# FFN middle of a two-layer decoder trunk: four parts in program order against five parts laid out by the kernel's own planner

## The chip, the cores and the metric

The kernel runs on one core of one Trainium2 chip. The metric is the device time of one execution in microseconds (us). Beside it stands one profiled execution, whose trace shows every instruction of the engines: TensorE (PE, with its weight loads as PEld), VectorE (DVE), ScalarE (ACT), GpSimd (POOL), and the DMA queues that SyncE (SP) and POOL issue.

## What is computed

Two layers of a decoder trunk, each a mixer (attention, two convolution groups, an output projection) followed by a feed-forward network (FFN). Only the FFN is touched:

```python
def ffn_sublayer(h, pre_g, post_g, w_up, conv_w, w_down):
    u = rms_norm(h, pre_g)
    z = jnp.einsum("bld,df->blf", u, w_up)
    z = causal_depthwise_conv(z, conv_w)
    g, up = jnp.split(z, 2, axis=-1)
    y = jnp.einsum("blf,fd->bld", jax.nn.silu(g) * up, w_down)
    return h + rms_norm(y, post_g)
```

The length is 528 (512 and 16 meta tokens), the model width 1024 (8 blocks of 128), the FFN width 2816, which is 22 blocks f of 128. For each f there is a gate half and an up half. All of it is float32, done as three matmuls on a high and a low part (hi times hi, hi times lo, lo times hi).

## The kernel before, in words

**Layout.** Channels lie on partitions, positions on the free axis. A weight block is loaded from DRAM into a raw tile (`raw` or `u`), ScalarE casts it to its high part (`whi`, `shi`, `ahi`), and VectorE subtracts to get the low part (`wlo`, `slo`, `alo`). A matmul takes 128x128 of such a weight and 264 columns of the right side (258 in the last layer, where some positions fall away). One product of 128 x 512 by 264 columns is 4 x 3 = 12 matmuls.

**Parts.** The 22 blocks are worked in parts (`PARTS`): 6, 6, 5, 5. In each part the up projections come first, then the gate (convolution taps, SiLU, product, split into `yhi` and `ylo`), and then the down projection: 8 output tiles m, each summing over the f of the part and added to `yp`. A down tile of a part of n blocks is 6n matmuls of 264 columns in layer 0 and 3n of 512 columns in layer 1.

**Seven products for eight.** The first part and the last block (f = 21) use plain up products. The 15 blocks f = 6 to 20 (`sevens`) cut the gate weight and the up weight into halves of 512 rows, and positions into two halves, so that eight block products become seven. The seven products of a block are a11, a12, s4, s2, a22, s3, s1 (`product`, `seven`, `p3`, `p4`), 84 matmuls in all. Their weights are sums of the loaded halves. The four sums are made by DMAs with an adding write, which POOL issues (`add1`, `add2`, `add3`): on the gate tile `raw` from DRAM, on the up tile `u` from DRAM, on `u` from `raw`, and on `raw` from `u`. The third needs the first, the fourth needs the third, and the gate tile must have been split before its first sum is added. After the sums, ScalarE and VectorE split the four results. There are two `u` tiles, and three `raw` tiles, which the down weights and the plain up weights use too. A `u` tile may be loaded again when its block's last sum has been added and its splits are done.

**The right sides.** t1, t2 and t4 are combinations of the pieces of the normed input, built during part 0 (`build_terms`). After the `yield "last"` t3 is built and the input itself, now scaled, is split again into `uhi` and `ulo`.

**What sets the order.** In this stretch the code is written in program order, with small pieces set ahead by hand (`ahead`, `AHEAD_STEPS`: load, split and add for the next block at named places), and a scheduler with a timeline then orders each engine's instructions at build time. Elsewhere (the mixer, and `finish`, which does the last part's down projection, the norm and the first products of what follows) the kernel uses its own planner, `Flow`: operations are given with an engine, a cost, what they wait for and a priority, matmul work is given as threads, and the planner simulates and so fixes the order (`manual_schedule`). Each engine, and each DMA queue, then works strictly in that order.

Lines of the profile: L648 are all matmuls of `mm3` (plain up and down products), L1978 those of the seven products. L1941/L1942 split the weights of the seven, L488/L489 other weights, L1915/L1916 split the input, L1998 to L2033 take the products out of PSUM into the z tiles, L1809 to L1836 are the convolution and gate, L2079/L2081 take the down tiles out, L1957/L1958/L1961/L1964 are the four adding DMAs.

## Time and profile before

| what | us |
|---|---|
| median of 3 runs | 1430.88 (1430.63 to 1435.54) |
| the profiled execution: its own time, its span | 1430.35, 1428.6 |
| PE busy, share of the span | 1289.2, 90% |
| layer 0, first down matmul of part 0 to last plain up product | 345.9 to 667.2 (321.3 long) |
| layer 1, the same | 1050.9 to 1372.4 (321.5 long) |
| DVE busy in the two stretches | 183.24 and 180.65 |
| ACT busy in the two stretches | 141.03 and 137.71 |

A row of the waits view gives engine, tile and line, what released it, and then the total, the number and the longest of the waits. A row of the timeline gives start, length, engine, line, operation, out<-in, shapes, and in brackets the idle time before it with what ended that. A row of the windows view gives the busy time of each engine with the number of instructions, then the granted TensorE clock as a share of full speed, the DMA share and GB/s. Matmuls overlap in the pipe, so one matmul's length in a row is longer than the distance between two.

### The profile page before, as it was taken

The page shows a single profiled execution, that of the slowest core. Times are in us where ns is not written, and L with a number is a line of the kernel's source. Part 1 is how long each engine was busy: PE and PEld are TensorE (multiplying, and loading weights), DVE is VectorE, ACT ScalarE, POOL GpSimd, SP SyncE. Part 2 cuts the span into 40 slices and gives each one's busy share as a digit, 9 for nine tenths or more (in the row PEclk, how much of TensorE's full clock was granted, in tenths as well). Part 3 has the DMA queues.
Part 4 walks back from the last instruction along what each step waited for, and adds up shares of the span by engine and source line. Part 5 has one row for each costly group of instructions (what it writes and reads, how often), then busy time and mean ns, then how long its engine had stood idle before and what let it go on. Part 6 is the DMA issues. An engine that isn't in the chain of part 4 may idle for free.

```text
span 1428.6 us, 24192 instructions
## 1 busy us (share of the span) xinstructions
PE 1289.2 (90%) x9390; PEld 1216.5 (85%) x9390; DVE 965.3 (68%) x1722; ACT 751.9 (53%) x1507; POOL 209.3 (15%) x387
## 2 busy tenths in 40 slices
PE   6999999999988889888989999999999788888886
PEld 6988989998988889888879898899978777777885
DVE  5688885799356546656666888668983555565565
ACT  7256677655344335345652566866553443443443
POOL 1312320000121021020003233100002110210200
PEclk9999999999999999999989999999999999999998
DMA  5133213432456366365240322153326653664641
GB/s 201 46 93 81 76 45 126 143 121 70 122 126 154 89 149 142 95 157 155 90 136 19 110 61 90 45 168 133 95 70 131 128 148 84 144 158 102 148 124 60
DMA packets 67219, 158.41 MB, mean 111 GB/s; under 512 B 7344, under 2 KB 21680, under 8 KB 66592
## 3 DMA queue, kind: packets, MB, share of 16 engines
q1 hardware_dynamic: 49184, 124.59, 27.1%
q0 software_dynamic: 17376, 31.73, 13.7%
q8 instruction: 74, 1.21, 0.4%
q10 hardware_dynamic: 544, 0.54, 0.1%
q14 instruction: 41, 0.34, 0.1%
HBM read 128.09 MB, written 8.65 MB: 96 GB/s over the span
## 4 chain that ended last, share of the span: by engine, by line
PE 47%; DMA 19%; DVE 14%; issue 8%; ACT 7%; POOL 4%; POOLq 0%; DVEq 0%; SPq 0%; ACTq 0%
PE psum L648 34%; DMA raw<-u 6%; DMA raw<-in_w_dram 6%; DMA u<-raw 4%; DMA u<-in_w_dram 3%; PE psum L1978 3%; PE psum L1397 2%; DVE c L1811 2%; PE psum L1146 2%; PE psum L1340 1%; PE psum L762 1%; DVE cacc L895 1%; DVE wlo L617 1%; ACT shi L1941 1%; POOL u L1961 1%
## 5 line engine op out<-in xcount | busy, mean ns | idle before, releaser
L648 PE MATMUL psum<-uhi,whi 128*128 128x264 f32 (+1 forms) x1024 | 276.1, 293 | 12.2 <-ACT uhi L805 10.1
L648 PE MATMUL psum<-ulo,whi 128*128 128x264 f32 (+1 forms) x1024 | 269.6, 287 | 1.9 <-DVE ulo L806 1.9
L648 PE MATMUL psum<-uhi,wlo 128*128 128x264 f32 (+1 forms) x1024 | 268.8, 286 | 0.0
L648 PE MATMUL psum<-yhi,whi 128*128 128x264 f32 (+3 forms) x824 | 237.5, 317 | 30.5 <-ACT yhi L1835 29.4
L648 PE MATMUL psum<-ylo,whi 128*128 128x264 f32 (+3 forms) x824 | 235.0, 311 | 2.3 <-DVE ylo L1836 1.8
L648 PE MATMUL psum<-yhi,wlo 128*128 128x264 f32 (+3 forms) x824 | 233.5, 309 | 0.7 <-DVE wlo L489 0.5
L648 PEld LDWEIGHTS psum<-uhi,whi 128*128 128x128 f32 x1024 | 185.6, 191 | 17.6 <-ACT uhi L805 10.9
L648 PEld LDWEIGHTS psum<-ulo,whi 128*128 128x128 f32 x1024 | 185.8, 191 | 2.9 <-DVE ulo L806 2.4
L648 PEld LDWEIGHTS psum<-yhi,whi 128*128 128x128 f32 x824 | 150.6, 195 | 44.1 <-ACT yhi L1835 31.9
L648 PEld LDWEIGHTS psum<-uhi,wlo 128*128 128x128 f32 x1024 | 185.7, 191 | 0.0
L648 PEld LDWEIGHTS psum<-ylo,whi 128*128 128x128 f32 x824 | 151.6, 195 | 11.1 <-DVE ylo L1836 4.3
L648 PEld LDWEIGHTS psum<-yhi,wlo 128*128 128x128 f32 x824 | 151.5, 194 | 7.4 <-DVE wlo L489 1.0
L1811 DVE SCALAR_TENSOR_TENSOR c<-z,pv,c 128x528 f32<-128x528 f32 (+1 forms) x176 | 130.5, 754 | 18.0 <-ACT c L1809 16.7
L617 DVE TENSOR_TENSOR wlo<-raw,whi 128x1024 fp32r<-128x1024 f32 (+2 forms) x86 | 99.2, 1168 | 34.9 <-ACT whi L613 34.7
L613 ACT CAST whi<-raw 128x1024 fp32r<-128x1024 f32 (+2 forms) x86 | 85.4, 1004 | 37.8 <-PE psum L648 21.9
L1942 DVE TENSOR_TENSOR slo<-raw,shi 128x512 fp32r<-128x512 f32 x60 | 40.8, 690 | 92.8 <-ACT shi L1941 88.2
L488 ACT CAST whi<-raw 128x768 fp32r<-128x768 f32 (+2 forms) x66 | 55.9, 846 | 87.1 <-PE psum L648 63.4
L1941 ACT CAST shi<-raw 128x512 fp32r<-128x512 f32 x60 | 35.6, 619 | 105.1 <-DMA raw<-u 70.5
L489 DVE TENSOR_TENSOR wlo<-raw,whi 128x768 fp32r<-128x768 f32 (+2 forms) x66 | 63.9, 969 | 36.8 <-ACT whi L488 34.7
L895 DVE SCALAR_TENSOR_TENSOR cacc<-apad,pv,cacc 128x528 f32<-128x528 f32 x120 | 87.6, 768 | 0.4
L1978 PE MATMUL psum<-h,shi 128*128 128x264 f32 (+1 forms) x240 | 53.5, 316 | 29.4 <-ACT shi L1941 21.3
L1941 ACT CAST shi<-u 128x512 fp32r<-128x512 f32 x60 | 37.0, 617 | 76.4 <-DMA u<-raw 76.0
(281 smaller groups left out, 3133.4 us busy)
## 6 DMA issues: line engine op xcount, KB each, us to landing
raw<-in_w_dram SPq DMA_DIRECT2D x114, 512.0 KB
u<-in_w_dram SPq DMA_DIRECT2D x30, 512.0 KB
raw<-in_w_dram SPq DMA_DIRECT2D x32, 384.0 KB
raw<-in_w_dram SPq DMA_DIRECT2D x32, 320.0 KB
u<-in_w_dram POOLq DMA_DIRECT2D x30, 256.0 KB, 4.0
raw<-in_w_dram POOLq DMA_DIRECT2D x30, 256.0 KB, 4.8
u<-raw POOLq DMA_DIRECT2D x30, 256.0 KB, 4.1
raw<-u POOLq DMA_DIRECT2D x30, 256.0 KB, 3.3
```

Of the source, the lines that this page charges most:

```text
L488: nc.scalar.copy(hi[:, :sz], raw[:, :sz])
L489: nc.vector.tensor_sub(lo[:, :sz], raw[:, :sz], hi[:, :sz].bitcast(F32))
L613: nc.scalar.copy(box["hi"][:, :sz], box["raw"][:, :sz])
L617: nc.vector.tensor_sub(lo[:, :sz], box["raw"][:, :sz], box["hi"][:, :sz].bitcast(F32))
L648: nc.tensor.matmul(d, lhsT=w[a][:, k, cols], rhs=rhs(b, k, hf), start=start and i == 0 and p == 0, stop=stop and i == n - 1 and p == 2)
L895: nc.vector.scalar_tensor_tensor(conv[j], in0=src, in1=conv[j], scalar=col("a_dw_w", CK * j + i), op0=ALU.mult, op1=ALU.add)
L1146: nc.tensor.matmul(ps[:n, :nw], lhsT=(uhi, ulo)[ui][:, k, P * b:P * b + n], rhs=w[wi][:, k % 4, :], start=k == 0 and p == 0, stop=k == KD ...
L1397: nc.tensor.matmul(acc[:, s0 - qa:qz - qa], lhsT=vt[:, b].rearrange("p h d -> p (h d)")[:, o:o + P], rhs=pt, start=b == 0 and i == 0, stop ...
L1811: nc.vector.scalar_tensor_tensor(dst, in0=src[:, i:i + 2 * fw], scalar=wtap(i, t), in1=dst, op0=ALU.mult, op1=ALU.add)
L1941: nc.scalar.copy(hi, raw)
L1942: nc.vector.tensor_sub(lo, raw, hi.bitcast(F32))
L1978: nc.tensor.matmul(d, lhsT=unit(f).a[a][i][:, P * k:P * (k + 1)], rhs=terms[b][j][k], start=start and k + p == 0, stop=k == KH - 1 and p = ...
```

## The change

The parts become 6, 3, 3, 3, 7. Everything from the end of part 0's plain products to `finish` is now laid out by the planner, in one plan with `finish`. Two threads feed PE: `ups`, the seven products of blocks 6 to 20 in the same order as before, and `downs`, the 8 down tiles of each of the first four parts, so one tile at a time. A list `goals` says after how many block products each down tile falls due: those of part 0 at 0, 0, 0, 0, 2, 5, 8, 11, and those of a later part spread evenly over the block products that follow its last block, the first 10 products later. A product waits while a due down tile can go. The weights, sums and splits of all 15 blocks are given to the planner at once, with priority by block. The tiles of the sums are kept and written again, instead of being allocated per block: each of s1 to s4 has one pair, a22 two, the gate split two, `u` two, gate raw three (one of them lent to part 0's down weights first), and down weights of the middle parts get one raw tile of their own (`draw`). t3 and the second split of the input, `late_terms`, are planned operations now. The last plain block and its gate run inside the same plan as `finish` (`last_up`). `finish` sums over 7 blocks instead of 5. The gate of block 5 is still scheduled by the build-time scheduler; the planner assumes it ready 7.5 us after its start. In the last layer 48 matmuls more are issued, since `finish` takes 2 x 256 columns where the middle takes 512.

```diff
-PARTS = (6, 6, 5, 5)
+PARTS = (6, 3, 3, 3, 7)
...
-                yield "last"
...
+            def late_terms():
...
+                terms["t3"] = [[t[k // 2][:, k % 2] for k in range(KH)] for t in t3]
+                plain_terms()
+                start, us = Tok(flow.now), 2 * sw
+
+                def unit_u(k):
+                    hi, lo, y = (t[:, k:k + 2, i0:] for t in (uhi, ulo, yp))
+                    n = 2 * (L - i0)
+                    a = act(act_us(n), lambda: nc.scalar.copy(hi, y), start, prio=0.1)
+                    return [a, dve(dve_us(n), lambda: nc.vector.tensor_sub(lo, y, hi.bitcast(F32)), a, prio=0.1)]
+
+                u_at = [unit_u(k) for k in range(0, KD, 2)]
+                ready_at["b11"], ready_at["b21"] = u_at[0] + u_at[1], u_at[2] + u_at[3]
...
+            sevens = list(range(PARTS[0], NF - 1))
+            ends = [sum(PARTS[:p + 1]) for p in range(len(PARTS))]
...
+                def __init__(self, f, bufs):
+                    self.a, self.box, self.at, self.slot = {}, {}, {}, {}
+                    box, src = self.box, [up_chunk(f, e) for e in range(2)]
+                    gs, us = Slot(), Slot()
+                    w = 1 + 0.001 * f
+                    lg = load_op(bufs["g"], gs, box, "g", src[0], 2 * HALF, w)
+                    lu = load_op(bufs["u"], us, box, "u", src[1], 2 * HALF, w)
+
...
+                    self.at["a11"] = self.at["a12"] = g2[1]
+
+                    def add(out, in_, *after):
+                        return gp(ADD_US, lambda: nc.gpsimd.dma_start(out(), in_(), accum_op=ALU.add), *after, prio=w, lat=ADD_LAT)
+
+                    def split(name, raw, *after):
+                        self.slot[name] = Slot()
+                        t = split_op(box, name, raw, after, bufs[name], self.slot[name], HALF, w)
+                        self.at[name] = t[1]
+                        return t
+
+                    a2 = split("a22", ub, lu)
+                    c1 = add(ua, lambda: src[1][:, HALF:], lu)
+                    c3 = add(ga, lambda: src[1][:, :HALF], *g2)
+                    c2 = add(ub, ga, c3, *a2)
+                    c4 = add(gb, ub, c2, *g2)
+                    s = {n: split(n, raw, c) for n, raw, c in (("s3", ga, c3), ("s1", ua, c1), ("s2", ub, c2), ("s4", gb, c4))}
+                    gs.close(s["s3"][1], s["s4"][1], c2)
+                    us.close(s["s1"][1], s["s2"][1], c4)
...
+            def ups(units, bufs):
+
+
+                def product(bank, f, a, b, *waits, start=False):
+                    u = units[f]
+                    yield [When(lambda: None if len(down_at) < due(counted[0]) and down_can() else [Tok(0.0)])]
+                    counted[0] += 1
+                    yield [u.at[a], *ready_at.get(b, []), *waits]
+                    d = psum[:, bank, :sw]
+                    w = u.weight(a)
+                    for k in range(KH):
...
+                def p3(f):
+                    d, tok = yield from product(banks_of(f)[0], f, "s4", "b22", done[f, "u4"])
+                    copied(f, "c12", 0, 1, d, tok)
+                    conv_flow(f, 0, [done[f, "c11"], done[f, "c12"]])
...
+                    zg, zu = (z_free.get((f - 2, e), []) for e in range(2))
+                    d, tok = yield from product(ba, f, "a11", "b11", *before(f - 2, "c12"), start=True)
+                    copied(f, "s1", 0, 0, d, tok, *zg)
+                    d, tok = yield from product(bc, f, "a12", "b21", *before(f - 2, "c11"), start=True)
+                    z = z_of(f, 0)[:, zin[0]]
+                    done[f, "c11"] = dve(vs, lambda z=z, d=d: nc.vector.tensor_add(z, z, d), tok, done[f, "s1"], prio=0)
+                    if prev is not None:
+                        yield from p3(prev)
+                    d, tok = yield from product(ba, f, "s2", "t2", done[f, "s1"])
+                    copied(f, "u2", 1, 0, d, tok, *zu)
+                    if prev is not None:
+                        yield from p4(prev)
+                    d3, tok3 = yield from product(bb, f, "s3", "t3", *before(f - 2, "c21"), start=True)
+                    d, tok = yield from product(ba, f, "s1", "t1", done[f, "u2"])
+                    copied(f, "u4", 1, 1, d, tok)
+                    less(f, "c22", 1, d3, tok3, done[f, "u4"])
+                    prev = f
+                y_last.append(tok)
+                yield from p3(prev)
+                yield from p4(prev)
+                over.add("ups")
...
+            counted, down_at, goals = [0], [], [0, 0, 0, 0, 2, 5, 8, 11]
+            for p in range(1, len(PARTS) - 1):
+                c0, n = 7 * (ends[p] - PARTS[0]) + 10, 7 * PARTS[p] + (3 if p == len(PARTS) - 2 else 0)
+                goals.extend(c0 + n * m // KD for m in range(KD))
+
+            def due(n):
+                return sum(x <= n for x in goals)
+
...
+            def downs(bufs, early):
+
+
+                pair = Ring(1)
+                for part, nf in enumerate(PARTS[:-1]):
...
+                        raw.close(a)
+                        if part == 0 and m == KD - 1:
+                            third.close(a)
...
+                        for group in (ks[:-1], ks[-1:]):
+                            for i, bank in enumerate((0, 5)):
+                                yield [blocks[i][1]]
+                                for k in group:
+                                    tok = yield from tile(i, bank, k)
+                                    yield
+                                if k == ks[-1]:
+                                    toks[i] = out(i, bank, tok)
...
+                        c_free.append(toks[1])
+                        m = 2
+                    for m in range(m, KD):
+                        yield [blocks[m][1], When(lambda: g_at.get(f0))]
+                        slot = yield from flow.grab(pair)
+                        for k in ks:
+                            tok = yield from tile(m, 0, k)
+                            yield
+                        pair_free[:] = [out(m, 0, tok)]
+                        slot.close(*pair_free)
+                        down_at.append(m)
+                        yield
+                over.add("downs")
+
...
+                for f in range(PARTS[0]):
+                    g_at[f] = [Tok(flow.now + (7.5 if f == PARTS[0] - 1 else 0.0))]
+                    z_free[f, 0] = z_free[f, 1] = [Tok(flow.now + (5.0 if f == PARTS[0] - 1 else 0.0))]
+                late_terms()
...
+                flow.thread(ups(units, bufs))
+                down_thread.append(downs(bufs, early))
+                flow.thread(down_thread[0])
...
+                flow.thread(last_up([x[2] for x in hl], hl), first=True)
+                if not final:
+                    plan_w(after_down, WE)
+                plan_w(len(chunks) if final else after_mixer[l + 1])
+                h, h_at = load_h(fp, h_mid[l], prio=3, after_all=[Tok(flow.now + 4)])
+                f0, nf = NF - PARTS[-1], PARTS[-1]
                 ks = list(range(nf))
```

What moves, at three places. On PE in layer 0, at the end of the up products of blocks 6 to 11, the order before is (`ahi`, `alo` are weights of the a22 product on the input term in `h`; `whi_5216` is a down weight, `yhi`, `ylo` are gated blocks):

```order
L1978 MATMUL psum_67<-h_3793,ahi_5149 128x264 x2
L1978 MATMUL psum_67<-h_3793,alo_5150 128x264
L648 MATMUL psum_67<-yhi_618_5306,whi_5216 128x264 x2
L648 MATMUL psum_67<-yhi_618_5306,whi_5222 128x264 x2
L648 MATMUL psum_67<-ylo_619_5307,whi_5216 128x264 x2
L648 MATMUL psum_67<-yhi_618_5306,wlo_5217 128x264 x2
L648 MATMUL psum_67<-ylo_619_5307,whi_5222 128x264 x2
```

From there on 240 down matmuls follow one another up to the next block product. In the change the down matmuls of a part of three blocks stand between two block products (`d0hi` is a down weight, `a221hi` and `s3hi` are weights of a22 and s3):

```order
L2124 MATMUL psum_67<-h_3793,a221hi_4343 128x264 x2
L2124 MATMUL psum_67<-h_3793,a221lo_4344 128x264
L644 MATMUL psum_67<-yhi_531_5087,d0hi_4272 128x264 x2
L644 MATMUL psum_67<-ylo_532_5088,d0hi_4272 128x264 x2
L644 MATMUL psum_67<-yhi_531_5087,d0lo_4273 128x264 x2
L2124 MATMUL psum_67<-acc_4196,s3hi_4397 128x264
L2124 MATMUL psum_67<-rs_4198,s3hi_4397 128x264
L2124 MATMUL psum_67<-acc_4196,s3lo_4398 128x264
```

So a down tile of 18 matmuls in layer 0 (three blocks) is cut in between products instead of 8 tiles in a row.

On POOL in layer 0, the adding DMAs around blocks 8 to 11 before (`u_4628` and `raw_4627` are block 8, `u_4765` and `raw_4764` block 9, 4902 and 4901 block 10, 5039 and 5038 block 11):

```order
L1961 DMA u_4628<-raw_4627 128x512
L1964 DMA raw_4627<-u_4628 128x512
L1958 DMA u_4902<-in_w_dram 128x512
L1961 DMA u_4765<-raw_4764 128x512
L1964 DMA raw_4764<-u_4765 128x512
L1957 DMA raw_5038<-in_w_dram 128x512
L1958 DMA u_5039<-in_w_dram 128x512
L1961 DMA u_4902<-raw_4901 128x512
L1964 DMA raw_4901<-u_4902 128x512
```

and in the change (`raw_4621` is block 8 and later block 11, `raw_4219` block 9, `raw_4252` block 10; `u_496` holds even blocks, `u_498` odd ones):

```order
L2029 DMA u_496_4236<-raw_4621 128x512
L2029 DMA raw_4621<-u_496_4236 128x512
L2029 DMA raw_4252<-in_w_dram 128x512
L2029 DMA u_498_4262<-raw_4219 128x512
L2029 DMA u_496_4236<-in_w_dram 128x512
L2029 DMA raw_4219<-u_498_4262 128x512
L2029 DMA raw_4621<-in_w_dram 128x512
L2029 DMA u_496_4236<-raw_4252 128x512
L2029 DMA u_498_4262<-in_w_dram 128x512
L2029 DMA raw_4252<-u_496_4236 128x512
```

Before, the second sum of block 10 (on `u_4902`) stands ahead of the third sum of block 9 (on `u_4765`). In the change that third sum (on `u_498`, from `raw_4219`) stands ahead of the second sum of block 10 (on `u_496`, from DRAM).

On DVE in layer 0, the gate of block 5 before (`c_4180` and `c_4185` are its two halves, `ylo_487` its low part, `rs` and `rz` hold low parts of t3, `wlo_4260` and the like are down weights):

```order
L1811 SCALAR_TENSOR_TENSOR c_4185<-z_377_2913,pv_2_68,c_4185 128x528
L1876 TENSOR_TENSOR rz_4197<-c_4202,acc_4195 128x528
L1831 TENSOR_TENSOR c_4180<-c_4180,c_4185 128x528
L1836 TENSOR_TENSOR ylo_487_4191<-c_4180,yhi_486_4190 128x528
L489 TENSOR_TENSOR wlo_4260<-raw_4257,whi_4259 128x768
L489 TENSOR_TENSOR wlo_4303<-raw_4300,whi_4302 128x768
L489 TENSOR_TENSOR wlo_4350<-raw_4347,whi_4349 128x768
```

and in the change (`ulo` are the four pieces of the input's low part, `d0lo` a down weight, `wlo_4289` and `a220lo` weights of block 6):

```order
L1929 TENSOR_TENSOR c_4217<-yp_2908 128x528
L1918 TENSOR_TENSOR ulo_112<-yp_2908,uhi_111 128x1056 x4
L1933 TENSOR_TENSOR rs_4198<-c_4209,acc_4196 128x528
L1807 SCALAR_TENSOR_TENSOR c_4185<-z_377_2913,pv_2_68,c_4185 128x528
L1933 TENSOR_TENSOR rz_4199<-c_4217,acc_4197 128x528
L1994 TENSOR_TENSOR d0lo_4273<-raw_4206,d0hi_4272 128x768
L1994 TENSOR_TENSOR wlo_4289<-raw_4219,whi_4288 128x1024
L1994 TENSOR_TENSOR a220lo_4300<-u_496_4236,a220hi_4299 128x512
L1827 TENSOR_TENSOR c_4180<-c_4180,c_4185 128x528
L1832 TENSOR_TENSOR ylo_487_4191<-c_4180,yhi_486_4190 128x528
```

The four pieces of `ulo`, one down weight and two weights of block 6 now stand ahead of the end of that gate.

More of the change, by code (lines that the diff above doesn't have):

```diff
@@ L48 @@
 WE = 0.5
+YS = 9
 NP = 3
@@ L480, in prep_one @@
             return
-        assert not by_seven(i)
         wpos[0] += 1
@@ L490, in prep_one @@
         ready.append((i, tuple(t[:, :sz].rearrange("p (k n) -> p k n", n=n) for t in (hi, lo))))
-    def by_seven(i):
-        return chunks[i][0] == "ffn_w_up" and PARTS[0] <= chunks[i][4][0][0] % DFF // P < NF - 1
     def prefetch(n):
         while wpos[0] < len(chunks):
-            if by_seven(wpos[0]) or wpos[0] not in wide and sum(i not in wide for i, _ in ready) >= n:
+            if wpos[0] not in wide and sum(i not in wide for i, _ in ready) >= n:
                 return
@@ L1966, in tile_hybrid_trunk @@
-            units = {}
-            def unit(f):
-                if f not in units:
-                    units[f] = Seven(f)
-                return units[f]
-            def product(bank, f, a, b, start=False):
-                d = psum[:, bank, :sw]
-                for k in range(KH):
-                    for p, (i, j) in enumerate(((0, 0), (0, 1), (1, 0))):
-                        nc.tensor.matmul(d, lhsT=unit(f).a[a][i][:, P * k:P * (k + 1)], rhs=terms[b][j][k],
-                                         start=start and k + p == 0, stop=k == KH - 1 and p == 2, skip_group_check=not start)
-                return d
@@ new lines, in tile_hybrid_trunk, with down_can @@
+            y_last, pair_free, over = [], [], set()
+            counted, down_at, goals = [0], [], [0, 0, 0, 0, 2, 5, 8, 11]
[4 more added lines that the diff above has]
+                return sum(x <= n for x in goals)
+            def down_can():
+                t = next((t for t in flow.threads if t[0] is down_thread[0]), None)
+                r = t and flow.ready(t[1])
+                return r is not None and r is not False and r <= flow.pe + 0.1
@@ L2041, in plain @@
                         continue
-                    if i < FIRST["w_out"]:
-                        scaled(i, [first.ps[hf, i] for hf in range(2)])
-                        continue
                     w = next_w()
```

473 lines of the change are left out of this document (287 added, 186 removed).

## The prediction

> **What bounds the kernel now.** I read the page's busy times first, then the chain that ended last, then the two FFN middles with the windows view, then what TensorE waits for in them.
>
> ```profile
> PE 1289.2 (90%) x9390; PEld 1216.5 (85%) x9390; DVE 965.3 (68%) x1722; ACT 751.9 (53%) x1507; POOL 209.3 (15%) x387
> PE 47%; DMA 19%; DVE 14%; issue 8%; ACT 7%; POOL 4%; POOLq 0%; DVEq 0%; SPq 0%; ACTq 0%
> ```
>
> TensorE is busy 90% of the span, yet it is only 47% of the chain. So over long stretches the chain runs through sums, splits and casts, and TensorE's share hides what is lost there. The middles (rows: window, length, then busy time and count of PE, PEld, DVE, ACT, POOL; granted clock, DMA share, GB/s) are:
>
> ```profile
> 345.90:667.20 321.30, 282.45 (x2137) 275.71 (x2136) 183.24 (x274) 141.03 (x247) 49.60 (x58) 0.94 0.53 123
> 1050.90:1372.40 321.50, 276.61 (x1730) 246.96 (x1729) 180.65 (x273) 137.71 (x248) 49.58 (x58) 0.95 0.54 124
> ```
>
> In these 322 us VectorE is 57% busy and DMA about half. Neither is a bound, so the question is how long the matmuls need. Distances between starts at a full clock, by the timeline: 264 columns, 25 rows of two; 258 columns, 32 rows; 512 columns, 11 rows.
>
> ```profile
> 374.90 0.40 PE L648 MATMUL psum<-yhi,whi 128*128 128x264 f32 x2
> ...
> 380.98 0.41 PE L648 MATMUL psum<-ylo,whi 128*128 128x264 f32 x2
> ...
> 1130.57 0.28 PE L1978 MATMUL psum<-ylo,shi 128*128 128x258 f32 x1
> ...
> 1134.41 0.28 PE L1978 MATMUL psum<-ulo,whi 128*128 128x258 f32 x1
> ...
> 1067.42 0.39 PE L648 MATMUL psum<-ylo,whi 128*128 128x512 f32 x1
> ...
> 1069.97 0.39 PE L648 MATMUL psum<-yhi,whi 128*128 128x512 f32 x1
> ```
>
> So a matmul takes 6.08/50 = .1216 us, 3.84/32 = .1200 and 2.55/11 = .2318. Layer 0's middle has 15 x 84 = 1260 matmuls of block products, 17 x 48 = 816 of down tiles and 96 of the last plain block: 2172 x .1216 = 264.1 us. It takes 321.3, so **57.2 us are lost**. Layer 1's has 1260 x .1200 + 408 x .2318 + 96 x .1200 = 257.3 of 321.5, a **loss of 64.2**. What TensorE waited for (total, times, longest), layer 0, then layer 1:
>
> ```profile
> PE psum L648 <- ACT yhi L1835: 11.1, 3, 4.1
> PE psum L1978 <- ACT z L2011: 8.1, 2, 4.6
> PE psum L1978 <- ACT shi L1941: 6.7, 6, 2.9
> PE psum L1978 <- ACT z L2021: 6.4, 4, 3.3
> PE psum L1978 <- ACT z L2032: 3.0, 3, 1.4
> ```
> ```profile
> PE psum L1978 <- ACT shi L1941: 17.9, 11, 4.3
> PE psum L648 <- ACT yhi L1835: 10.8, 4, 4.4
> PE psum L1978 <- ACT z L2021: 9.7, 6, 3.4
> PE psum L1978 <- ACT z L1998: 2.8, 3, 1.2
> PE psum L1978 <- ACT z L2032: 2.6, 2, 1.4
> ```
>
> These add up to 35.3 and 43.8 us. Three kinds are in them: the gate at the head of each part's down tiles (yhi), the first products after a lump of down tiles, and the sums of the seven (shi) with the results that must leave PSUM (z). The rest of the loss is a lower clock behind gaps. Two matmuls behind gaps of 4.12 and 2.67 us, and the windows view of TensorE alone after them (length, busy, clock, DMA share, GB/s):
>
> ```profile
> 479.89 1.05 PE L648 MATMUL psum<-yhi,whi 128*128 128x264 f32 x4 [4.12 <-ACT yhi L1835]
> ...
> 1101.83 0.58 PE L1978 MATMUL psum<-yhi,shi 128*128 128x258 f32 x1 [2.67 <-ACT z L2021]
> ```
> ```profile
> 480.00:484.00 4.00, 4.00 (x19) 0.57 0.00 0
> ...
> 1101.00:1106.00 5.00, 4.17 (x24) 0.66 0.96 153
> ```
>
> After 4.12 us of idleness 4 us run at .57, so 4 x .43 = 1.7 us go; after 2.67 us 5 us run at .66, again 5 x .34 = 1.7. By the waits' rows some seven gaps a layer are 2.7 us or longer (three gates, three restarts, one shi): 12 of the 22 and 20 us that these rows leave unexplained.
>
> The sums are slow because of a POOL order. The chain of waits around block 9:
>
> ```profile
> 419.76 3.24 DMA raw<-u
> 423.07 3.37 DMA u<-in_w_dram
> ...
> 428.74 3.56 issue
> 432.31 3.32 DMA raw<-u
> ...
> 441.27 7.38 DMA u<-raw
> ...
> 448.94 3.27 DMA raw<-u
> ```
>
> From fourth sum to fourth sum pass 12.6 and 16.6 us. An unmixed block has 84 x .1216 = 10.2 us of matmuls, so here the sums set the pace, and TensorE catches up and waits. During the lumps of down tiles the sums run ahead, but only as far as two u tiles allow.
>
> **The change, part by part.** *The same work in another place.* The matmul count stays; 96 matmuls (two blocks, 8 tiles; 11.7 us) move from each middle into finish, which is neutral. In layer 1 half-width matmuls replace 512-wide ones there: 2 x .1200 for .2318, under .5 us, taken as 0. Four parts instead of three give 8 more evacuations a layer:
>
> ```profile
> L2081 DVE TENSOR_TENSOR yp<-yp,psum 128x528 f32<-128x528 f32 x16 | 11.2, 701 | 16.9 <-PE psum L648 16.9
> ```
>
> 8 x .70 = 5.6 us of VectorE beside its 138 idle us in a middle: nothing. Without that cover it is 5.6.
>
> *Dealing out.* From about block 10 on a mixed block holds 84 + 48 = 132 matmuls, 16.05 us, against cycles of 12.6 and 16.6 for the sums. The third sum, now ahead of the next block's second on POOL, shortens the cycle where blocks come unmixed. So about 10 blocks a layer have cover and 5 (blocks 7 to 10 in the main, and the last) have not. For those I keep today's wait per block. The L1978 rows sum to 24.2 and 33.0 us; three restarts of about 3 us each a layer leave 39 over 30 blocks, 1.3 us a block. The residual is 5 x 1.3 = 6.5, then 10 mixed blocks at .3 (an estimate: the small waits, a quarter of today's) = 3, and two dips of the clock = 3.4: **13 us** a layer, with ends 3 (a sum always ahead) and 25 (all 15 blocks at 1.3, and three dips). The gates of parts now come a whole block before the part's first down tile is due, so those waits vanish.
>
> *A new stall at the start.* Part 0's first down tiles have 60 matmuls before they need block 5's gate: 7.3 us from 345.9, to 353.2. Before:
>
> ```profile
> 343.83 2.42 DVE L1916 TENSOR_TENSOR ulo<-yp,uhi 128x1056 fp32r<-128x1056 f32 x2
> 349.25 0.95 DVE L489 TENSOR_TENSOR wlo<-raw,whi 128x768 fp32r<-128x768 f32 x1
> 353.33 0.51 PE L648 MATMUL psum<-ylo,whi 128*128 128x264 f32 x2 [0.95 <-DVE ylo L1836]
> 357.83 1.25 PE L648 MATMUL psum<-yhi,whi 128*128 128x264 f32 x4 [3.25 <-ACT yhi L1835]
> 370.84 1.23 DVE L1942 TENSOR_TENSOR wlo<-raw,whi 128x1024 fp32r<-128x1024 f32 x1 [3.59 <-ACT whi L1941]
> ```
>
> VectorE worked without a break up to that gate, at 357.8. In the change d0lo (.95), wlo (1.23) and a220lo (half that size, .68) stand ahead of it, 2.85 us, less the .95 of the row at 349.25, which stood there too. The 2.42 of the pieces of ulo at 343.83 now wait for the last up product, so they too fall in this stretch. The gate comes 1.9 + 2.4 = 4.3 us later, at 362.1, and TensorE idles 362.1 - 353.2 = 8.9 instead of 4.2. With 1.7 of clock that is **10.7 us** in layer 0, and I take the same in layer 1, where the order is the same. Ends: 6 (the pieces fit into the earlier gaps) and 13.
>
> *The heads of finish.* The last part's first wait, and the wait for the next stage's first products:
>
> ```profile
> 676.79 0.39 PE L648 MATMUL psum<-yhi,whi 128*128 128x264 f32 x1 [3.72 <-ACT yhi L1835]
> 722.87 0.59 PE L648 MATMUL psum<-uhi,whi 128*128 128x264 f32 x1 [6.10 <-ACT uhi L805]
> 1381.80 0.58 PE L648 MATMUL psum<-yhi,whi 128*128 128x256 f32 x1 [3.78 <-ACT yhi L1835]
> ```
>
> Six blocks instead of four stand ready ahead of the last gate: 72 matmuls cover it for 48, 2.9 us more. The gaps shrink to about .9 each and keep the clock up: (3.72 + 1.7) + (3.78 + 1.7) - 1.7 = 9.2 gained; ends 0 (the gate comes later by as much) and 11. At 722.87 some of the second half's added matmuls, 36 x .1216 = 4.4 us, stand under the norm: I take 3 of 0 to 4.4.
>
> *Sum.* 1430.35 - (57.2 - 10.7 - 13) - (64.2 - 10.7 - 13) - 9.2 - 3 = 1344. The profiled execution lies .5 under the median, so the forecast is **1345 us**. With the ends of the terms (residual -10 to +12 and start -4.7 to +2.3 per layer, finish 11 to 0) and not all at once: 1330 to 1362.
>
> The Trainium skill ("TensorE: Matmul & The Clock Gate", Part 1: The HAM clock gate) says that TensorE falls to half rate only after an idle window of about 3.4 us. By that rule the two dips of my residual, behind gaps under 3.4 us, would cost nothing, and the sum would be 2 x 3.4 = 6.8 lower, 1338. The trace has .66 behind 2.67 us and disagrees; I go by the trace.
>
> **The rivals.** *Nearly all stalls go.* The sums keep ahead everywhere (residual 3 a layer) and the start costs no more than 8: 1345 - 20 - 5 = 1320. For it: POOL is busy only 50 of 322 us, and all splits now have a priority by block. Against: an unmixed block of 10.2 us is shorter than any cycle seen. Chance .17.
>
> *VectorE's order keeps the pace.* VectorE works strictly in the planned order, and each of its waits for a cast, a sum or a PSUM result delays all behind it. It is busy (183.2 + 5.6)/15 = 12.6 us a block, and idled 138/15 = 9.2. My forecast leaves a middle 276 long (321.3 - 33.5 - 11.7), so 5.8 idle a block. If 7.5 stay, halfway, each middle is 15 x 20.1 = 302: 26 longer, 1345 + 51 = 1396; a quarter of the way gives 1370. For it: the one gate that I followed already comes later by such an order. Chance .22.
>
> *It pays nothing.* Every down tile that is due but whose part's gate or weight is late holds up the products behind it, and the lump's waits come back as small ones in the same total: 1424 to 1438. Against: the cover of a mixed block. Chance .05.
>
> *Slower: the adding DMAs collide with the down weights.* The sum at 441.27 took 7.38 us instead of 3.3. Now down weights are loaded throughout, among the sums. If fourth sum, load and third sum each take 7.38, the cycle is 12.6 + 4.1 + 4.0 + 3.8 = 24.5 us; my mixed blocks need 16.05 + .3. It decides from where the 85 us gained are eaten by 20 mixed blocks: 16.35 + 4.3 = 20.6, that is two of the three at 7.38 in every mixed block. All three: 1345 + 20 x 8.1 = 1507. Against: DMA is at .53 of its share, and the down loads are the same bytes. Chance .08.
>
> **How the numbers follow.** Forecast .48, nearly all .17, VectorE's order .22, nothing .05, slower .08. The likeliest one's own range is 1330 to 1362. To leave out no more than 2 in 10, I go to 1314 below (nearly all of the second) and 1396 above (most of the third). Half a per cent, 7 us, is about what a measurement of this kernel can tell from no change. Faster by more: .48 + .17 + .22 = .87; within it .05; slower .08.
>
> **What would show it.** In the changed profile: middles of about 276 us at a clock of .97 or more; no waits on yhi but one gap of about 9 us in the first down tiles of each layer, and VectorE busy up to it; L1978's waits for shi and z down to some 10 us a layer, most of them in blocks 7 to 10; the distance between fourth sums under 16 us in the mixed blocks; heads of finish under 1 us; the wait at L805 near 3. If that first gap is 5 or less, the start is mis-sized. If the middles exceed 290 and VectorE's waits for casts have grown, it was its order; if the sums take 7 us regularly, the collision. The forecast is wrong if the middles stay above 300.

## The result, and the profile after

The changed kernel takes **1315.3 us** (1314.32 to 1316.64, 4 runs) against 1431.03: a ratio of .9185, 95% interval .9164 to .9206. That is 30 us under the forecast of 1345, below the range of the outcome that I held likeliest (1330 to 1362) and just inside the whole range (1314 to 1396). By the number it is the rival that nearly all stalls go (1320), which I had given a chance of .17; by its terms it is not, as the account below shows. Its profiled execution took 1316.64 (span 1314.9), 113.7 us less than the 1430.35 of before.

The page's busy times after:

```profile
PE 1247.1 (95%) x9438; PEld 1190.0 (90%) x9438; DVE 979.4 (74%) x1754; ACT 756.2 (58%) x1525; POOL 211.1 (16%) x387
```

TensorE is busy 95% of a shorter span. The windows view of the middles, from the first down matmul to the first of finish (columns as in the prediction), of the changed kernel:

```profile
344.70:613.40 268.70, 256.34 (x2078) 254.44 (x2077) 198.09 (x302) 146.15 (x265) 49.44 (x58) 0.99 0.66 153
992.60:1258.20 265.60, 252.86 (x1718) 233.32 (x1717) 194.07 (x304) 145.64 (x265) 49.43 (x58) 0.98 0.68 156
```

and of the kernel before, now cut at the same two events:

```profile
345.90:671.80 325.90, 287.05 (x2174) 280.31 (x2173) 187.56 (x281) 143.07 (x251) 49.60 (x58) 0.94 0.53 125
1050.90:1376.80 325.90, 281.01 (x1766) 251.36 (x1765) 184.43 (x280) 140.05 (x252) 49.58 (x58) 0.95 0.54 124
```

The second pair shows a slip of mine. The windows on which the prediction rests ended at 667.2 and 1372.4, and their rows held 2137 and 1730 matmuls, where I multiplied 2172 and 1764: about 36 of the last plain block came later. With all of them the loss before was 325.9 - 264.1 = 61.8 and 325.9 - 257.3 = 68.6 us, 9 us more than I had to give away. After, 2076 x .1216 = 252.4 of 268.7 in layer 0 and 1260 x .1200 + 360 x .2318 + 96 x .1200 = 246.2 of 265.6 in layer 1 are matmuls at full pace: 16.3 and 19.4 are lost.

What TensorE waits for in the two middles after (total, times, longest):

```profile
PE psum L644 <- ACT yhi L1831: 7.3, 1, 7.3
PE psum L2124 <- DVE s2lo L1994: 1.8, 2, 1.4
PE psum L2124 <- ACT z L2137: 1.6, 2, 1.1
PE psum L644 <- ACT yp L2285: 0.7, 1, 0.7
PE psum L2124 <- ACT s2hi L1991: 0.6, 1, 0.6
```
```profile
PE psum L644 <- DVE ylo L1832: 3.9, 2, 2.4
PE psum L644 <- ACT yhi L1831: 3.5, 1, 3.5
PE psum L644 <- DVE yp L2287: 2.3, 1, 2.3
PE psum L2124 <- DVE s2lo L1994: 1.8, 2, 1.0
PE psum L644 <- ACT yp L2285: 0.7, 1, 0.7
PE psum L2124 <- ACT z L2137: 0.5, 1, 0.5
```

The block products (L2124) wait 4.0 and 2.3 us, where they (L1978) waited 24.2 and 33.0. What is left is mostly block 5's gate at the start. One wait in layer 1 is of another kind: a down tile waited for the evacuation of the one before it (yp L2287). On VectorE that evacuation stood behind the split of a weight, for whose cast VectorE itself had waited 2.08 us. The matmul, and the granted clock in the 4 us after it:

```profile
1086.08 0.50 PE L644 MATMUL psum<-yhi,whi 128*128 128x512 f32 x1 [2.27 <-DVE yp L2287]
...
1086.08:1090.08 4.00, 4.00 (x15) 0.57 0.88 152
```

Why the old waits belonged together is seen from ScalarE. What ScalarE waited for in layer 0 before, the rows of the casts of the sums (shi):

```profile
ACT shi L1941 <- DMA u<-raw: 38.7, 15, 5.5
ACT shi L1941 <- DMA raw<-u: 31.4, 15, 3.2
ACT shi L1941 <- DMA raw<-in_w_dram: 18.2, 6, 7.1
```

and its timeline at the restart after part 0's down tiles, before, with the matmul that waited:

```profile
395.94 0.62 ACT L1941 CAST shi<-raw 128x512 fp32r<-128x512 f32 x1 [7.13 <-DMA raw<-in_w_dram]
396.46 0.61 ACT L1941 CAST shi<-u 128x512 fp32r<-128x512 f32 x1
396.98 0.37 ACT L2011 COPY z<-psum 128x264 f32<-128x264 f32 x1
...
397.40 0.81 PE L1978 MATMUL psum<-h,shi 128*128 128x264 f32 x2 [4.58 <-ACT z L2011]
```

ScalarE stood 7.13 us before the cast of a sum that had not landed, and the copy of z out of PSUM stood behind that cast in its order. TensorE's wait is booked to z, but it was a wait for a sum. After, the same view of ScalarE has, of the sums, only

```profile
ACT s4hi L1991 <- DMA raw<-u: 1.3, 1, 1.3
ACT s2hi L1991 <- DMA u<-raw: 0.4, 1, 0.4
```

The sums did not get faster for it. POOL's issues of the fourth sum after, of blocks 8 and 9 (those of blocks 10 to 12 follow at 434.85, 448.51 and 462.38):

```profile
406.91 0.85 POOL L2029 DMA_DIRECT2D raw<-u  x1 [4.01 <-DMA u<-raw]
...
422.45 0.84 POOL L2029 DMA_DIRECT2D raw<-u  x1 [3.65 <-DMA u<-raw]
```

Those of blocks 8 to 11 lie 15.5, 12.4 and 13.7 us apart, much as before (12.6 and 16.6). But TensorE now has work between them. Down matmuls alone (L644) in those stretches, by the windows view:

```profile
422.45:434.85 12.40, 0.00 (x0) 1.00 0.87 182
434.85:448.51 13.66, 4.86 (x36) 1.00 0.75 174
448.51:462.38 13.87, 4.71 (x36) 1.00 0.80 183
```

Only up to 434.85, some two blocks, is there no down tile; the products wait 2.0 us there and 1.4 in the stretch behind it, in gaps of at most 1.44, and the granted clock stays at 1.00.

### The profile page after: what moved, and what is told of

It reads as the page before. It is cut to its first block, busy times and chain, and to the rows that moved or that the text cites. A ratio compares the mean times of both kernels' runs of the same rounds, so it can differ in the third digit from the quotient of the medians.

```text
span 1314.9 us, 24357 instructions
## 1 busy us (share of the span) xinstructions
PE 1247.1 (95%) x9438; PEld 1190.0 (90%) x9438; DVE 979.4 (74%) x1754; ACT 756.2 (58%) x1525; POOL 211.1 (16%) x387
## 5 line engine op out<-in xcount | busy, mean ns | idle before, releaser
L644 PE MATMUL psum<-uhi,whi 128*128 128x264 f32 (+1 forms) x1024 | 274.0, 292 | 5.2 <-ACT uhi L801 5.0
L644 PE MATMUL psum<-ulo,whi 128*128 128x264 f32 (+1 forms) x1024 | 267.9, 286 | 1.8 <-DVE ulo L802 1.8
L644 PE MATMUL psum<-uhi,wlo 128*128 128x264 f32 (+1 forms) x1024 | 267.2, 285 | 0.0
L644 PE MATMUL psum<-yhi,whi 128*128 128x264 f32 (+3 forms) x678 | 193.8, 302 | 15.5 <-ACT yhi L1831 10.8
L644 PE MATMUL psum<-ylo,whi 128*128 128x264 f32 (+3 forms) x678 | 191.0, 298 | 4.2 <-DVE ylo L1832 3.9
L644 PEld LDWEIGHTS psum<-uhi,whi 128*128 128x128 f32 x1024 | 184.6, 190 | 10.1 <-ACT uhi L801 5.9
L644 PE MATMUL psum<-yhi,wlo 128*128 128x264 f32 (+3 forms) x678 | 190.3, 297 | 0.1
L644 PEld LDWEIGHTS psum<-ulo,whi 128*128 128x128 f32 x1024 | 184.8, 190 | 2.9 <-DVE ulo L802 2.4
L644 PEld LDWEIGHTS psum<-uhi,wlo 128*128 128x128 f32 x1024 | 184.7, 190 | 0.0
L644 PEld LDWEIGHTS psum<-yhi,whi 128*128 128x128 f32 x678 | 124.1, 190 | 21.9 <-ACT yhi L1831 11.5
L644 PEld LDWEIGHTS psum<-ylo,whi 128*128 128x128 f32 x678 | 124.0, 190 | 8.6 <-DVE ylo L1832 5.0
L644 PEld LDWEIGHTS psum<-yhi,wlo 128*128 128x128 f32 x678 | 124.3, 190 | 3.5 <-DVE wlo L613 0.5
L2064 DVE SCALAR_TENSOR_TENSOR c<-z,pv,c 128x528 f32<-128x528 f32 (+1 forms) x128 | 96.9, 758 | 9.3 <-ACT c L2062 8.1
L2137 ACT COPY z<-psum 128x264 f32<-128x264 f32 (+2 forms) x120 | 45.1, 376 | 75.3 <-PE psum L2124 74.3
L1994 DVE TENSOR_TENSOR wlo<-raw,whi 128x1024 fp32r<-128x1024 f32 (+1 forms) x40 | 47.3, 1183 | 30.3 <-ACT whi L1991 30.1
L2124 PE MATMUL psum<-uhi,whi 128*128 128x264 f32 (+1 forms) x240 | 68.1, 284 | 0.0
L2124 PE MATMUL psum<-uhi,wlo 128*128 128x264 f32 (+1 forms) x240 | 68.0, 283 | 0.0
L2124 PE MATMUL psum<-ulo,whi 128*128 128x264 f32 (+1 forms) x240 | 68.0, 283 | 0.0
```

The source lines that it names most:

```text
L644: nc.tensor.matmul(d, lhsT=w[a][:, k, cols], rhs=rhs(b, k, hf), start=start and i == 0 and p == 0, stop=stop and i == n - 1 and p == 2)
L1994: return a, dve(dve_us(n), lambda: nc.vector.tensor_sub(box[name][1], raw(), box[name][0].bitcast(F32)), a, prio=prio)
L2064: nc.vector.scalar_tensor_tensor(c, in0=z[:, i:i + n], scalar=wtap(i, t), in1=c, op0=ALU.mult, op1=ALU.add)
L2124: nc.tensor.matmul(d, lhsT=w[i][:, P * k:P * (k + 1)], rhs=terms[b][j][k], start=start and k + p == 0, stop=k == KH - 1 and p == 2, skip_g ...
L2137: done[f, name] = act(us, lambda: nc.scalar.copy(z_of(f, e)[:, zin[h]], d[:, lo:]), *after, prio=0)
```

## The experiments

The runs were made in three groups, each on a chip of its own, with the kernel before beside them (1427.7 to 1429.2 in the three). The changed kernel unedited ran in one of them and is the measure for the others:

> The changed kernel once more, unedited, as the measure for the runs beside it: 1310 to 1318 us, .9185 of the kernel before.

1314.48 us, before 1427.69, ratio .9204 (.919 to .9218). Differences below are to this.

**The parts alone.** In the kernel before:

```diff
-PARTS = (6, 6, 5, 5)
+PARTS = (6, 3, 3, 3, 7)
```

> The kernel before with the parts 6, 3, 3, 3, 7 alone, in program order. If the part sizes by themselves carry the gain: 1380 us or less. If dealing out and planning do: finish gets shorter by its 7 blocks (up to 19 us in both layers together), but each layer has one more part's head with a gate, a restart and two dips of the clock (about 10 us), so 1420 to 1440.

1432.73 against 1427.8, ratio 1.0033 (1.0017 to 1.0049). The part sizes are worth nothing by themselves. What finish gains (the wait of 6.10 for the next stage's first products is 1.1 there), the additional part's head takes; TensorE waits for five gates there with finish's, 19.8 us in layer 0 (before four, 11.1 + 3.7).

**The sums left out, in both kernels.** Before:

```diff
-            AHEAD_STEPS = {..., "add1": [("add1",)], ..., "add2": [("add2",)], ... ("add3",)], ...}
+            AHEAD_STEPS = {..., "add1": [], ..., "add2": [], ...}
```

and in the changed kernel the planned operation stays, without its DMA:

```diff
-return gp(ADD_US, lambda: nc.gpsimd.dma_start(out(), in_(), accum_op=ALU.add), *after, ...)
+return gp(ADD_US, lambda: None, *after, ...)
```

> The kernel before without the four adding DMAs of each block (the sums are left out, so the products use plain weights; all else is computed). It tells what the sums cost there. If they cost what I took (1.3 us in 30 blocks, and some dips of the clock): 1375 to 1395. If the lumps' gates and restarts are most of the loss: above 1400. If the sums lie behind nearly all of the 120 us lost in the middles: 1340 or less.

> The changed kernel, its order of everything else kept, without the four adding DMAs of each block (left out as in the run beside it). If the sums are covered but for the unmixed blocks 8 to 10: 4 to 10 us under the changed kernel. If they still cost elsewhere, by collisions with the loads: 15 us or more.

1340.64 against 1429.21 (ratio .9384, .9369 to .9398): **the sums cost the kernel before 88.6 us**, more than twice the 39 and some dips that I took. The changed one takes 1312.09, 2.4 us under 1314.48. By the ratios (.9178 against .9204, whose intervals just overlap) it is 3.7. They cost it next to nothing, no more than the 4 I expected at least. Without the sums the middles of the kernel before still have two gates each, waits of TensorE in layer 0:

```profile
PE psum L648 <- ACT yhi L1835: 7.4, 2, 3.7
PE psum L1978 <- DVE rz L1876: 1.8, 1, 1.8
```

The restarts after lumps, and every wait for z above .3 us, are gone with the sums. So they were the sums' waits, as ScalarE's order suggested. (The build-time scheduler may order other work differently without the adding DMAs, and the DMA load is less; the 88.6 holds both.)

**Down tiles crowded.** All eight tiles of a later part fall due together:

```diff
-                goals.extend(c0 + n * m // KD for m in range(KD))
+                goals.extend(c0 for m in range(KD))
```

> The changed kernel, but each later part's eight down tiles all fall due at once (10 products after its last block) instead of evenly, so they alternate with some 8 products, and about 13 of each 21 products follow one another with no down tile between. Theory A (the dealt-out down matmuls give the sums their time): the blocks without cover go from about 5 to about 11 a layer, at 1.2 us each and two more dips of the clock of 1.7: 10 us a layer, 1335 us. Theory B (it is the planned order of loads, sums and splits that takes the waits away, whatever stands between the products): 1313 to 1319.

1354.9 against 1427.8, ratio .9482 (.9446 to .9517): 40 us slower than dealt out. Theory A has the sign and half the size. Theory B does not hold: only the due times were touched, though the planner lays the other engines out anew around them. The two middles are 18.5 us longer each. In layer 0 (287.2 long) the sums' rows come back, and the evacuation of one down tile before the next appears beside them:

```profile
PE psum L644 <- DVE yp L2287: 4.6, 3, 2.6
PE psum L2124 <- DVE s2lo L1994: 3.9, 6, 1.4
PE psum L2124 <- ACT s2hi L1991: 3.4, 4, 1.5
```

I had priced an uncovered block at 1.2 us, about half of what the rows allow: the cycle of the sums less the products, 12.4 - 10.2 = 2.2 us and more, once their lead is used up.

**POOL's order put back.** The third sum of a block has to follow the next block's sum on u (the second run lets it go once that is issued, not landed):

```diff
-                    c2 = add(ub, ga, c3, *a2)
+                    c2 = add(ub, ga, c3, *a2, When(lambda: [units_c1[f + 1]] ...))
+                    units_c1[f] = c1
```

> The changed kernel, but the third sum of every block has to follow the next block's first sums on POOL, as it did before. If that order set the cycle of the sums (12.6 us against 10.2 us of products), the 5 unmixed blocks a layer lose 2.4 us each, 12 a layer and some clock: about 1343 us; mixed blocks of 16 us lose nothing. If the order on POOL doesn't matter: 1313 to 1319.

> As the POOL-order run that took 1420.7 us, but the planner holds the third sum only until the next block's sum on u is issued, not until it has landed. Theory C (the queue order itself costs it: the third sum stands behind a sum that waits for a u tile to be freed, loaded and summed, so two blocks' chains follow one another): cycles of 18 us and more stay, 1390 us or more. Theory D (the planner's extra wait did it; the order alone gives the 12.6 to 16.6 us of the kernel before, under the 16 us of a mixed block): 1320 to 1350.

The first took 1420.7 (ratio .9951, .9933 to .9969), the second 1346.38 (.9429, .9415 to .9443). So the order on POOL, with the plan that is made around it, is worth **32 us** here (theory D), and 74 of the first run's 106 came from the longer hold that I gave the planner. The likely reason, which I did not follow in the trace, is that it then plans every engine around sums that it believes late. In the second run the fourth sums lie 15.5 us apart where TensorE has hardly a down tile, and 15.9 and 16.4 in the next two blocks:

```profile
428.09 1.00 POOL L2031 DMA_DIRECT2D raw<-u  x1
...
443.64 1.19 POOL L2031 DMA_DIRECT2D raw<-u  x1
```

A mixed block of 16 us has just that time; an uncovered one loses 5. With the changed order the shortest cycle, past the first two blocks, is 11.8 to 12.4 in the two profiles of the changed kernel.

**POOL's order alone, in the kernel before.**

```diff
+                    third_sum[self.f] = nc.gpsimd.dma_start(self.ub, self.ga, accum_op=ALU.add).ins
...
+                        with tc.issue_after(third_sum[self.f - 1]):
+                            nc.gpsimd.dma_start(self.ua, self.src[1][:, self.HALF:], accum_op=ALU.add)
```

> The kernel before, with one thing of the change: on POOL each block's third sum goes ahead of the next block's sum on u. In the changed kernel the old order cost 32 us. If the order is worth the same beside lumps of down tiles: 1390 to 1405 us. If the lumps' gates and restarts take it back: above 1412.

1417.43 against 1429.21, ratio .9928 (.9904 to .9952): 11.8 us, as the second theory had it. TensorE's waits for shi fall from 6.7 to 1.8 us in layer 0, but those for gates rise from 14.8 (finish's included) to 17.1, and those for z from 17.5 to some 21:

```profile
PE psum L648 <- ACT yhi L1835: 17.1, 5, 4.8
PE psum L1984 <- ACT z L2027: 8.8, 5, 3.8
PE psum L1984 <- ACT z L2017: 7.3, 4, 2.4
...
PE psum L1984 <- ACT shi L1943: 1.8, 3, 0.9
```

**VectorE loaded more.** Each low part of the four sums is subtracted twice:

```diff
-                    s = {n: split(n, raw, c) for ...}
+                    s = {n: twice(n, raw, split(n, raw, c)) for ...}
```

> The changed kernel, but VectorE subtracts each low part of the four sums twice, to the same values: 4 x .69 = 2.8 us more of VectorE a block, 41 us a layer, known to the planner. If VectorE has room (12.6 of some 17 us a block were its work): under 10 us in all, 1315 to 1325. If VectorE's strict order is what keeps the pace: at least half of it shows, 1355 or more.

1348.57 against 1427.8 (.9449, .9419 to .9478): 34 us appear of the 82 that I counted as added, between the two theories. VectorE's busy time in the two middles grew by less than I counted, by 32.0 and 34.9 us (198.1 to 230.1 and 194.1 to 229.0), so half of what was really added appears. In layer 0 VectorE is not what sets the pace (the middle is 6.7 us longer); in layer 1 it nearly is (24.2 longer), with waits for s2lo:

```profile
PE psum L2129 <- DVE s2lo L2038: 11.1, 7, 2.5
```

**Down weights loaded twice.**

```diff
+                            if part:
+                                nc.sync.dma_start(box["raw"].rearrange("p (m s) -> p m s", m=n), src)
                             nc.sync.dma_start(box["raw"].rearrange("p (m s) -> p m s", m=n), src)
```

> The changed kernel, but every down weight of the middle parts is loaded twice into its tile (the planner doesn't know of the second): 24 x 192 KB more a layer beside the sums. If the sums collide with loads (third sum well above its median of 3.7 us, cycles above the 16 us of a mixed block): 10 us slower or more than the changed kernel. If DMA has the room that its share of .65 shows: within 5 us.

1385.57 against 1429.21 (.9695, .9677 to .9713), 71 us slower, but not for the reason that was to be tested. The landing times of the third and fourth sums by the DMA view (KB each, median us to landing):

```profile
u<-raw POOLq DMA_DIRECT2D x30, 256.0 KB, 4.2
raw<-u POOLq DMA_DIRECT2D x30, 256.0 KB, 3.5
```

The changed kernel has 3.7 and 3.5 there: the third sum takes .5 longer, the fourth as long as before. What grew is ScalarE's wait for the down weight itself, in layer 0 from 15.4 + 10.1 us to

```profile
ACT whi L1991 <- DMA draw<-in_w_dram: 49.5, 12, 6.2
ACT d0hi L1991 <- DMA draw<-in_w_dram: 28.1, 8, 5.4
```

There is one raw tile for the middle parts' down weights, so a load can't begin before the last has been split, and ScalarE and VectorE stand in order before its cast. The experiment doubled the loading in that chain. It says nothing on whether more bytes through another tile would collide; it does show that the one tile has not the time of a second load to spare.

**The start.** The pieces of ulo are planned 9.8 us after the start:

```diff
-                start, us = Tok(flow.now), 2 * sw
+                start, late, us = Tok(flow.now), Tok(flow.now + 9.8), 2 * sw
...
-... nc.vector.tensor_sub(lo, y, hi.bitcast(F32)), a, prio=0.1)
+... nc.vector.tensor_sub(lo, y, hi.bitcast(F32)), a, late, prio=0.1)
```

> The changed kernel, but the four pieces of ulo may go on VectorE only 9.8 us after the plan's start, so that they stand behind the end of block 5's gate. If those pieces are what makes that gate late, TensorE's waits of 7.3 us in layer 0 and of 3.5 + 2.4 in layer 1 shrink by 4.8 us each, with the dip of the clock in layer 0: 8 to 13 us less than the unedited kernel. If the first block products then wait for ulo instead: no difference, within 3 us.

1314.92 (.9203, .9184 to .9223): no difference. The gate is no longer late, but the stall moves. Timeline of TensorE in layer 0:

```profile
354.25 0.51 PE L644 MATMUL psum<-yhi,whi 128*128 128x264 f32 x2 [0.27 <-ACT yhi L1831]
356.61 0.51 PE L644 MATMUL psum<-ylo,whi 128*128 128x264 f32 x2 [1.85 <-DVE ylo L1832]
360.68 0.59 PE L2124 MATMUL psum<-ulo,whi 128*128 128x264 f32 x1 [2.24 <-DVE ulo L1918]
364.49 0.81 PE L644 MATMUL psum<-yhi,d0hi 128*128 128x264 f32 x2 [1.02 <-ACT yp L2285]
```

7.34 us in one wait become 5.4 in four. So the pieces of ulo do delay the gate, as predicted, and this order gains nothing: their 4.75 us on VectorE are then what the first products wait for.

**Seven blocks in finish.** Five instead:

```diff
-PARTS = (6, 3, 3, 3, 7)
+PARTS = (6, 4, 4, 3, 5)
```

> The changed kernel with the parts 6, 4, 4, 3, 5: finish sums over 5 blocks as before, and 96 matmuls of each layer come back into the middle, which is neutral by itself. If the 7 blocks of finish cover its heads as I worked out (9 us for the gates, 3 for the next stage's first products): 12 us slower than the unedited kernel. If the planner covers them anyway, since the last gate is in its plan: within 4 us.

1329.25 (.9318, .93 to .9335), 14.8 us slower than the unedited kernel, where I had 12. The next stage's first products wait again as they did before (6.10):

```profile
675.73 0.59 PE L644 MATMUL psum<-uhi,whi 128*128 128x264 f32 x1 [5.80 <-ACT uhi L801]
```

But the gates that the kernel before waited for in finish (3.72 and 3.78) do not come back: with five blocks too TensorE has no wait for yhi there. By the profiles 8.4 us of the loss lie in finish, and 4.2 in the middle of layer 0, where down tiles wait 4.4 us for evacuations (0.4 in the changed kernel).

## Why the prediction was right in sign and too high

The miss is 30 us, 27.5 of them between the sum and the profiled execution. The terms below give 27.2 of these: 9 for the loss before, 10 for the residual, 1.7 for the start and 6.5 for finish. By the steps of the prediction:

- **The loss to be won was too small by 9.** "It takes 321.3, so 57.2 us are lost": the windows left out 36 matmuls that I counted as done in them. The count stood in the quoted rows.
- **The residual, 13 a layer.** The mechanism, cover by dealt-out tiles, was right (40 us by the crowded run; some 85 us of the sums' cost hidden). The size was not: the uncovered blocks of "5 x 1.3" were about two, and all block products together waited 4.0 us in layer 0 and 2.3 in layer 1. Of the two dips of the clock layer 0 had none behind its start, where no gap exceeds 1.5 us. Layer 1 had one, behind the 2.27 us at 1086.08: a wait for an evacuation, which the prediction put at "nothing". Layer 0 loses 16.3; the start has 7.34 + .69 of waits and 4 us at .58, 1.7, so 9.7; the rest is 6.6. In layer 1 the start has 1.5 + 3.5 + 2.4 + .7 us of waits and about 2 of clock, 10 in all, so the rest is 9.4, of which that evacuation and its dip are 4.0.
- **The start, 10.7 a layer.** About 9.7 and 10: right, and the place was right, down to the pieces of ulo that ran ahead of the gate. One long gap, as forecast, is in layer 0 only; in layer 1 the wait is in three (1.50, 3.46 and 2.37). The rows of layer 0 (4.76 us of ulo, then the gate):

```profile
348.93 4.76 DVE L1918 TENSOR_TENSOR ulo<-yp,uhi 128x1056 fp32r<-128x1056 f32 x4
...
359.54 0.81 PE L644 MATMUL psum<-yhi,whi 128*128 128x264 f32 x2 [7.34 <-ACT yhi L1831]
```

- **The heads of finish, 9.2 + 3.** From the first matmul of finish to the next stage's first product layer 0 takes 50.6 us instead of 51.0, with 11.7 us of matmuls more in it, so 12.1 gained; layer 1, to the end, 56.7 instead of 51.8 with 11.5 more: 6.6. Together 18.7, against 12.2 forecast. The step behind the 9.2 failed, though. I had it that "72 matmuls cover it for 48". The wait at 676.79 stood behind only 9 matmuls of finish, since the late gate was not the last block's but block 20's (the two casts of yhi are at 676.10 and 679.75). Seven blocks do not cover it: in the kernel before with the new parts it is longer,

```profile
672.06 0.59 PE L648 MATMUL psum<-yhi,whi 128*128 128x264 f32 x1 [5.46 <-ACT yhi L1835]
```

and in the changed kernel with five blocks it is gone: as the planner ordered it, that cast runs at 617.50, well before finish starts at 629.23. That run gives the division: with five blocks finish takes 46.5 instead of 51.0 us in layer 0 and 46.0 instead of 51.8 in layer 1, so 10.3 come from the plan; that this is near 9.2 is luck. The two blocks more gain the other 8.4, most of it the wait of 6.10 that went to 1.09 (I had 3 of it). Its dip of the clock did not go: the 4 us from 664.02 run at .50 after too. What is left at the gates' place are waits of 1.18 and 1.28 for an evacuation (L1593). The row that answers to 722.87:

```profile
664.02 0.59 PE L644 MATMUL psum<-uhi,whi 128*128 128x264 f32 x1 [1.09 <-ACT uhi L801]
```

- **The reading of the waits.** I booked gates, restarts and sums as three kinds and priced the sums at 1.3 us in 30 blocks. The runs without sums show that restarts and z's were the sums too: 88.6 us. The rows that show it, ScalarE's waits, were in the trace of before; the prediction does not use them.

Of the rivals, that nearly all stalls go has the number but not the terms: it had 3 us of residual a layer and a start of 8, where 6.6 and 9.4 and about 10 were measured, and the greater loss before and the greater gain of finish made up for that. VectorE's order does not keep the pace in layer 0, but nearly does in layer 1 (6.7 and 24.2 us of 32.0 and 34.9 added). The collision of sums and down loads did not show in the sums' median landing times (3.5 to 5.3 us by kind, not 7.38), and a test of it alone is missing. That it pays nothing is out. The check "fourth sums under 16 us apart in mixed blocks" was a wrong sign to look for: some lie over 19 us apart. From 462.38 to 589.96 the mean of eight cycles is 15.9, beside the 16.05 us of matmuls of a mixed block, so TensorE, no longer waiting, is what the cycle seems to follow.

By the runs the 113 us are divided so: some 85 from the sums, 19 from finish (10 of them by the plan, 8 by its two blocks more), and the rest from the middles' gates less the new start. No single part brings the 85: the part sizes alone 0, POOL's order alone 12; taking the order back costs 32, taking the dealing out back 40. What the planned loads and splits and the kept tiles bring by themselves no run separates.

## What to carry to other kernels

A wait that the profile books to one producer may be a wait of that producer's engine for something else that stands ahead in its order: before pricing kinds of waits apart, read what the releasing engine waited for. A slow chain of DMAs need not be made faster where its cycle (here 12 to 16 us) can be matched by putting other work of the busiest engine between its users in even portions; check the portion against the cycle, block by block. And compare the count of instructions in a window's row with the count by which you multiply.

## What the runs showed of the hardware

The clock's dips begin behind shorter gaps than I took (2.67 us). In the kernel before with POOL's new order a gap of 2.38 us at 403.10 leaves the next 4 us at full clock, one of 2.56 at 462.59 does not:

```profile
403.10:407.10 4.00, 4.00 (x33) 1.00 0.76 260
462.59:466.59 4.00, 2.35 (x13) 0.62 0.46 132
```

Between 340 and 672 us of the two kernels and of four experiments (crowded, splits twice, loads twice, and this one) all 15 gaps of 2.56 to 4.12 us were followed by 4 us at .50 to .64; of the ten of 1.7 to 2.4, five by 1.00 and five by .59 to .72 (two of these with a further gap of about 1 us close behind). The Trainium skill ("TensorE: Matmul & The Clock Gate", Part 1: The HAM clock gate) puts the limit at an idle window of about 3.4 us, free-running; the rows disagree with the length. In the new residual one gap lies in that range, the 2.27 us at 1086.08 in layer 1, with .57 behind it: about 1.7 us of the sum.
